# The first block's HGRN values of all heads, computed first and with tokens on partitions

## The chip, the cores and the metric

The kernel runs on one core of one Trainium2 chip. The metric is the device time of one execution in microseconds (us); the median of several runs counts. A difference of 0.2%, which is 4.8 us here, is about the least that can be told from no change. The engines go by the profile's names: PE (TensorE, with its weight loads as PEld), DVE (VectorE), ACT (ScalarE), POOL (GpSimd) and SP (SyncE, whose queue issues every DMA of this kernel).

## The reference: what is computed

One encoder layer is applied to a prompt of 512 tokens and to a sample of 1024 tokens, with 1024 channels, all in fp32. Cut to what matters here:

```python
h = rms_norm(x, n_pre_mix)                 # x * rsqrt(mean(x^2)) * gain, per token
proj = h @ w_in                            # 1024 x 6672
qkv_g, z_g, a_g, b_g, q_h, f_h, i_h, g_h, gate_raw = split(proj)
# Gated DeltaNet, 4 heads, both directions: conv + silu on q,k,v; l2norm;
#   per chunk a triangular inverse; a state that is carried over the chunks
# HGRN2, 4 heads, both directions:
ih = to_heads(i_h, HG_HEADS)               # the values v of the recurrence
# S_t = diag(f_t) S_{t-1} + k_t v_t^T,  o_t = S_t^T q_t
o_b = gla_chunked(qh, kh[0], ih, logf[0]) + flip_seq(gla_chunked(...))
merged = gates_a * (o_a @ w_br_gdn) + gates_b * (o_b @ w_br_hg)
x = x + rms_norm(merged @ w_out, n_post_mix)
h2 = rms_norm(x, n_pre_ffn)
return x + rms_norm((silu(h2 @ w_gate) * (h2 @ w_up)) @ w_down, n_post_ffn)
```

`i_h` is the projection that the change is about. It is used linearly, with no activation.

## The kernel before, in words

**Blocks.** Tokens are handled in three blocks of 512: sequence 0 is block 0 (the prompt), sequence 1 is blocks 1 and 2. K, the 1024 input channels, is cut into eight parts of 128 (`KD = 8`). A projection of 128 output columns over one block is 24 matmuls of 128x128 weights against 512 moving columns: eight parts of K by three products (`mm3`: high by high, high by low, low by high). Each fp32 operand is split into a rounded high part (an activation on ACT) and the rest (a subtraction on DVE); the helper is `split`. The result has channels on partitions and tokens in the free dimension, in one PSUM bank of eight.

**The first block.** `prelude(q)` loads the transposed input `xt` in eight parts of 256 KB, scales each by the norm's gain and splits it into `hi` and `lo` (`ha_a` in the profile). These are not yet divided by the token's root mean square. Projections that run on them are called raw: their eviction waits until the sums of squares over tokens are known (`pl.mark(("rstd", 0))`), and multiplies by the row `rstd[0]`. The sums of squares and the small decay products (`ab_products`) are 128-row, 32-column matmuls on PE; in the plan they stand behind the line `yield ("at", TOKENS)`. The activations that square the inputs (`sq`), a few constants (`constants()`, `ab_constants()`) and the splitting of the first weights share ACT and DVE with the splitting of `xt`. Weights come by `fetch`, 512 KB each; `AHEAD` says behind which part of the input the first of them are issued: z of head 0 (1536) behind part 0, q of HGRN (2064) behind part 1, the values (3600) behind part 4.

**The values before.** In `dense(q)` each head has its own projection `C_IH + h * P`, with `cbv` as its eviction: a copy of the bank to `iT`, and later `transp`, four 128x128 transposes on PE and a copy from the bank, so that tokens stand on partitions. `hg_post` uses the result (`out["v"]`) as the moving operand, `hg_mix` as weights.

**Streams.** Five generators write the program in an order that a planner (`Plan.run`) decides with its own rough clock: the prelude, the Gated DeltaNet stream (`gdn`), the HGRN stream, the dense stream (all plain projections and the 16 gate projections of a sequence), and the second phase. For each Gated DeltaNet head there is a chain: K projection, convolution on DVE, Gram matrix, a 31-step inverse on POOL (`inverse`, fed through DRAM tile `u_sc`), merges, then the recurrence. Dense projections fill PE meanwhile. Keys hold some of them back: a gate of group k needs Gated DeltaNet head k-1, and the gates past `HOLD[q][k]` of a group wait for `("inv", q, k)`, set late in the inverse of head k. `TRIG` names the inverse after which the sample's prelude starts.

**The order on the engines.** `Tape` records all operations and `schedule` orders them by a model of the engines and DMAs. On each engine, the ready operation with the lowest number comes first; an operation that is ready is never held back for a better one that isn't. The emitted order per engine is fixed; the hardware then runs each queue in that order. `URGENT` moves weight splits ahead in that numbering, `NEAR` bounds how far a matmul of the same form may be pulled ahead, `NW` is the number of buffers for split weights (4 KB a partition each). Every operation is emitted from one line of the file, so all of the trace has line 649; tiles tell the operations apart: `la_a`, `ba_a`, `sm_a`, `sa_a` hold fp32 data, `wa_a` split weights, `ha_a` split inputs, `bank` PSUM.

The second phase (branches, output projection, FFN) follows and is not touched but for `NW` and `NEAR`.

Of the kernel before, what the change touches and what calls it, by code (L numbers as in the profile page):

```python
# [13 lines left out]
F32 = mybir.dt.float32  # L14
F32R = mybir.dt.float32r
I32 = mybir.dt.int32
AF = mybir.ActivationFunctionType
# [4 lines left out]
P = 128  # L22
D = 1024
KD = D // P
# [9 lines left out]
C_Z, C_A, C_QH, C_FH, C_IH, C_GH, C_GATE = 1536, 2048, 2064, 2576, 3600, 4112, 4624  # L34
QSCALE = 128.0 ** -0.5
TBUFS = 8
NW = 6
NH = NFF // 2
MIXER = ("ones", "offd", "m_all", "m_b", "mbd", "wab0", "wab1")
RBUFS = 1  # L40
WBUFS = (2, 2, 2)
HOLD = ((2, 2, 2, 2), (2, 2, 2, 2))
MSTEP = (24, 28)
PAIR = False
SKEW = 24
URGENT = 100
PO = False
NVEC = 88
AHEAD = {0: 1536, 1: 2064, 4: 4112 - 512}
TRIG = 2  # L50
TOKENS, NORMED = 10.0, 30.0
QSQ = P * EPS ** 0.5
EPSQ = P * EPS * EPS

# [108 lines left out]
class Tape:  # L163
# [7 lines left out]
    SWITCH = 110  # L171
    FULL = (P, P)
    ENTER = 55
    NEAR = 300
    GROUP = 4
    AHEAD = 500
    RATE = 260.0
# [585 lines left out]

@with_exitstack
def layer(ctx, tc, x_p, x_s, w_out, n_post_mix, n_post_ffn, w_down, vec, xt_p, xt_s, w_in, w_br, w_gate, w_up,
          w_ab, y_p, y_s):
    tc.nc.scalar.preload_act_table_set("natural_log_exp_and_others")
    nc = Tape(tc.nc)
    w_out, w_down = w_out[0], w_down[0]
# [11 lines left out]
    def act(out, in_, func, **kw):  # L781
        nc.scalar.activation(out, in_, func, **kw)
        pl.op("ACT", out, aps(in_, kw.get("bias"), kw.get("scale")))
        if kw.get("accum_out") is not None:
            pl.ready[pl.key(kw["accum_out"])] = pl.ready[pl.key(out)]
# [20 lines left out]
    def stt(out, a, s, b, op0, op1):  # L806
        nc.vector.scalar_tensor_tensor(out, a, s, b, op0, op1)
        pl.op("DVE", out, aps(a, s, b))
# [126 lines left out]
    def h_tiles():  # L935
        return [pl.tile(hp, [P, KD, TB], F32R, n, n, 2) for n in ("h_hi", "h_lo")]
# [63 lines left out]
    def blk(name):  # L1000
        return pl.tile(tp, [P, TB + 4], F32, name, "t", TBUFS)[:, 0:TB]
# [92 lines left out]
    class Seq:  # L1094
        def __init__(self, si, b0, nb):
            self.si, self.b0, self.nb = si, b0, nb
            self.nt, self.L, self.ni = nb * 4, nb * TB, nb * 8
            self.n_i = 4 * self.ni
            self.hT = []
            self.ab = {}  # L1100
            self.late = None
            self.z = {}
            self.hg = [dict() for _ in range(HEADS)]

    def rstd_row(blk_):
# [47 lines left out]
    def prelude(q):  # L1153
        def load(b, k):
            xt = gt_("xt", 8)
            src = (xt_p if q.si == 0 else xt_s)[k * P:(k + 1) * P, b * TB:(b + 1) * TB]
            dma(xt, src)
            return xt

        def normed(b, k, xt, hi, lo, eng=None):  # L1160
            stt(xt, xt, g_mix[:, k:k + 1], rstd[q.b0 + b], ALU.mult, ALU.mult)
            split(hi[:, k, :], lo[:, k, :], xt, eng)
        if q.si == 0:
            xt = []
            for k in range(KD):
                xt.append(load(0, k))
                if k in AHEAD:
                    ahead[AHEAD[k]] = fetch(AHEAD[k])
                if k == 3:
                    for i in range(2):  # L1170
                        dma(wab[i].rearrange("p k m -> p (k m)"), w_ab[:, i * P:(i + 1) * P])
            hi, lo = h_tiles()
            for k in range(KD):
                act(hi[:, k, :], xt[k], AF.Copy, scale=g_mix[:, k:k + 1])
                stt(lo[:, k, :], xt[k], g_mix[:, k:k + 1], hi[:, k, :].bitcast(F32), ALU.mult, ALU.subtract)
            q.hT.append((hi, lo))
            pl.done["h", 0, 0] = 0.0
            constants()
            ab_constants()
            yield ("at", TOKENS)  # L1180
            sq = [blk("sq") for k in range(KD)]
            pn = px()
            for k in range(KD):
                act(sq[k], xt[k], AF.Square)
            for k in range(KD):
                for c in range(4):
                    mm(pn[32 * c:32 * c + 32, 0:P], ones[:, 0:32], sq[k][:, c * P:(c + 1) * P], k == 0, k == KD - 1)
            ab_products(q, 0, xt, range(KD))
            r = sblk("r4")
            act(r, pn[:, 0:P], AF.Ln, bias=eps_c, scale=1.0 / D)  # L1190
            act(r, r, AF.Exp, scale=-0.5)
            ab_scaled(q, 0, r)
            row = blk("row")
            tt(t4(row), r[:, None, :].to_broadcast([P, 4, P]), ident[:, 0:P:32][:, :, None].to_broadcast([P, 4, P]), ALU.mult)
            pn = px()
            nc.apart()
            mm(pn, ones, row)
            row = blk("row")
            copy(row, pn)
            q.late = rstd[0] = row  # L1200
            pl.mark(("rstd", 0))
            while waiting:
                waiting.pop(0)()
            yield ("at", NORMED)
            hi, lo = h_tiles()
            for k in range(KD):
                yield ("at", NORMED + 10 * k)
                normed(0, k, xt[k], hi, lo)
            q.hT[0] = (hi, lo)
            q.late = None  # L1210
        else:
            for b in range(q.nb):
                yield from rstd_row(q.b0 + b)
                xt = [load(b, k) for k in range(4)]
                if b:
                    yield need(("dense", 0))
                hi, lo = h_tiles()
                for k in range(KD):
                    if k % 4 == 0:
                        yield pl.at(*xt[k:k + 4])  # L1220
                        ab_products(q, b, xt, range(k, k + 4))
                    if k < 4:
                        xt.append(load(b, k + 4))
                    normed(b, k, xt[k], hi, lo)
                    yield 0
                ab_scaled(q, b)
                q.hT.append((hi, lo))
                pl.mark(("h", q.si, b))
        pl.mark(("pre", q.si))
# [427 lines left out]
    def dense(q):  # L1657
        for h in range(HEADS):
            st = q.hg[h]
            st.update({"sf0": {}, "sf1": {}, "q": {}, "v": {}})  # L1660

            def zcb(key):
                q.z[key] = {}

                def cb(ps, b):
                    s = blk("sg")
                    sigm(s, ps)
                    q.z[key][b] = ht_("zs", 2)
                    tt(q.z[key][b], ps, s, ALU.mult)
                return cb  # L1670

            def cbq(ps, b, st=st):
                s = blk("sg")
                sigm(s, ps)
                st["q"][b] = ht_("hq", 2)
                stt(st["q"][b], ps, QSCALE, s, ALU.mult, ALU.mult)

            def cbv(ps, b, st=st):
                iT = blk("sg")
                copy(iT, ps)  # L1680
                st["v"][b] = ht_("hv", 2)
                return lambda: transp(st["v"][b], iT)

            def cbf(d, st=st):
                def cb(ps, b):
                    st["sf%d" % d][b] = ht_("sf", 4)
                    sigm(st["sf%d" % d][b], ps)
                return cb

            def hgk(i):  # L1690
                return ("hg", 0, HEADS + i) if i < 0 and q.si else (("hg", q.si, i) if i >= 0 else ("h", q.si, 0))
            zk = hgk(h - 1)
            hk = hgk(h - 1 if q.si else h - 2)
            dep = ("h", q.si, 0)
            if not (h and q.si == 0):
                yield (zk, dep, ("gdn", 0, 3) if q.si else dep), C_Z + h * P, zcb(("z", h)), ("z", q.si, h)
            yield (hk, dep), C_QH + h * P, cbq, None
            yield (hk, dep), C_IH + h * P, cbv, None
            yield (hk, dep), C_FH + h * P, cbf(0), None
            yield (hk, dep), C_FH + 512 + h * P, cbf(1), ("hgin", q.si, h)  # L1700
            if h and q.si == 0:
                yield (zk, dep), C_Z + h * P, zcb(("z", h)), ("z", q.si, h)
            yield (zk, ("gdn", q.si, h) if q.si else dep), C_GH + h * P, zcb(("G", h)), ("G", q.si, h)
# [51 lines left out]
    def hg_stream():  # L1755
        for q in seqs:
            for h in range(HEADS):
                yield need(("hgin", q.si, h), ("gdn", q.si, h))
                yield from hg_attn(q, h)
                yield need(("G", q.si, h))  # L1760
                yield from hg_mix(q, h)
                pl.mark(("hg", q.si, h))
                yield 0
# [819 lines left out]
def _layouts(a):  # L2583
# [15 lines left out]
    for c in range(4):  # L2599
# [7 lines left out]
            'w_branch': np.ascontiguousarray(np.concatenate(br, axis=2)),  # L2607
            'w_gate': _tiles(np.asarray(a['w_ffn_gate'])[0]),
            'w_up': _tiles(np.asarray(a['w_ffn_up'])[0]),
            'w_ab': ab.reshape(P, KD * 32)}  # L2610


_LAY = ('vec', 'xt_prompt', 'xt_sample', 'w_in', 'w_branch', 'w_gate', 'w_up', 'w_ab')


# [13 lines left out]
```

## Time and profile before

| | |
|---|---|
| median of 3 runs | 2384.22 us (2383.85 to 2384.77) |
| profiled execution, its own time | 2382.66 us |
| span of its trace | 2381.0 us, 37933 instructions |
| PE busy | 2362.8 us (99%), 14183 matmul records |
| PEld / DVE / ACT / POOL busy | 83% / 73% / 52% / 32% |
| first matmul starts at | 8.01 us |
| last matmul group ends at | 2373.6 us |
| DMA | 42.6% of 16 engines' span, 141 GB/s |

A timeline row gives the start in us, the time in us from the first start to the last end of the rows that were merged, the engine, line and operation, the tiles written and read, the shape and the count; brackets tell how long the engine had been idle and what ended that. A waits row gives the total idle time, how often, and the longest. A windows row gives, for one stretch, each engine's busy time and instruction count, the granted PE clock, the busy share of the DMA engines and the rate. A chain row gives the start and length of a piece of the chain of waits that ended last.

### The profile page before, as it was taken

What the parts mean: (1) busy time and instruction counts of PE and PEld (TensorE: products, weight loads), DVE (VectorE), ACT (ScalarE), POOL (GpSimd) and SP (SyncE); (2) the same over time, 40 slices, a digit from 0 to 9 for tenths busy, and PEclk for the clock granted to TensorE, in tenths of its full rate; (3) what the DMA queues carried; (4) which work ended last, traced back from release to release, by engine and by line L of the source; (5) the groups of instructions that cost most, each with busy time, mean ns of one, the idle gap of its engine ahead of it and who ended that gap; (6) DMA issues with size and microseconds to landing.
All of it is one profiled execution on the core that took longest, in us unless ns stands there. A gap on an engine that the chain in (4) does not pass through costs nothing.

```text
span 2381.0 us, 37933 instructions
## 1 busy us (share of the span) xinstructions
PE 2362.8 (99%) x14183; PEld 1974.6 (83%) x14183; DVE 1727.0 (73%) x2826; ACT 1239.0 (52%) x2159; POOL 755.4 (32%) x1019
## 2 busy tenths in 40 slices
PE   8999999999999999999999999999999999999998
PEld 7888888888888888888888888888888888888887
DVE  8777898857857968758766984755887877544566
ACT  6656776746637547548442464545354444433343
POOL 0623435241602612502310011114666774200221
PEclk9999999999999999999999999999999999999999
DMA  5242643221330321324873463552454544674463
GB/s 199 95 145 63 218 143 101 95 66 46 101 96 18 100 83 54 96 78 148 299 261 133 159 221 110 163 170 84 168 192 175 187 170 160 213 246 137 148 206 125
DMA packets 193496, 337.72 MB, mean 142 GB/s; under 512 B 53185, under 2 KB 92961, under 8 KB 193313
## 3 DMA queue, kind: packets, MB, share of 16 engines
q1 hardware_dynamic: 193312, 335.31, 42.6%
q8 instruction: 111, 1.82, 0.3%
q14 instruction: 73, 0.59, 0.1%
HBM read 254.59 MB, written 80.66 MB: 141 GB/s over the span
## 4 chain that ended last, share of the span: by engine, by line
PE 90%; DVE 2%; DMA 1%; ACT 1%; SPq 0%; issue 0%; POOL 0%; DVEq 0%; ACTq 0%; POOLq 0%
PE bank L649 90%; DVE la_a L649 1%; DMA ba_a<-lay_w_in 1%; DVE ba_a L649 1%; ACT la_a L649 0%; SPq L649 0%; DMA ba_a<-x_sample 0%; DVE wa_a L649 0%; ACT ba_a L649 0%; ACT wa_a L649 0%; DMA dram_g_sc<-la_a 0%; ACT sm_a L649 0%; DMA la_a<-dram_u_sc 0%; DVE sm_a L649 0%; POOL la_a L649 0%
## 5 line engine op out<-in xcount | busy, mean ns | idle before, releaser
L649 PE MATMUL bank<-ha_a,wa_a 128*128 128x512 f32 x5424 | 1307.7, 395 | 8.4 <-ACT wa_a L649 8.0
L649 PEld LDWEIGHTS bank<-ha_a,wa_a 128*128 128x128 f32 x5424 | 1003.7, 188 | 210.1 <-ACT wa_a L649 8.0
L649 PE MATMUL bank<-xr_a 128*128 128x512 f32 x1386 | 314.3, 389 | 0.0
L649 PEld LDWEIGHTS bank<-xr_a 128*128 128x128 f32 x1386 | 260.1, 188 | 54.0
L649 PE MATMUL bank<-xr_a,ha_a 128*128 128x512 f32 x1200 | 275.3, 389 | 0.0
L649 PEld LDWEIGHTS bank<-xr_a,ha_a 128*128 128x128 f32 x1200 | 225.2, 188 | 46.8
L649 POOL TENSOR_TENSOR ba_a<-ba_a 128x512 f32<-128x512 f32 (+1 forms) x123 | 159.8, 1305 | 219.0 <-ACT wa_a L649 79.9
L649 ACT ACTIVATE la_a<-la_a 128x512 f32<-128x512 f32 (+1 forms) x307 | 194.4, 649 | 42.5 <-DVE la_a L649 30.7
L649 DVE TENSOR_TENSOR wa_a<-la_a,wa_a 128x1024 fp32r<-128x1024 f32 (+1 forms) x121 | 142.0, 1184 | 59.7 <-PE bank L649 28.3
L649 ACT ACTIVATE wa_a<-la_a 128x1024 fp32r<-128x1024 f32 (+1 forms) x121 | 118.3, 986 | 106.2 <-PE bank L649 97.7
L649 DVE TENSOR_TENSOR wa_a<-ba_a,wa_a 128x1024 fp32r<-128x1024 f32 (+1 forms) x103 | 123.6, 1218 | 68.7 <-PE bank L649 57.5
L649 ACT ACTIVATE wa_a<-ba_a 128x1024 fp32r<-128x1024 f32 (+1 forms) x103 | 99.3, 980 | 118.5 <-PE bank L649 94.9
L649 ACT ACTIVATE ha_a<-ba_a 128x512 fp32r<-128x512 f32 (+1 forms) x126 | 80.7, 642 | 135.7 <-PE bank L649 109.9
L649 POOL TENSOR_TENSOR la_a<-la_a 128x256 f32<-128x256 f32 (+1 forms) x80 | 89.4, 1133 | 183.1 <-DVE la_a L649 67.9
L649 DVE TENSOR_TENSOR ha_a<-ba_a,ha_a 128x512 fp32r<-128x512 f32 (+1 forms) x126 | 127.9, 1020 | 13.4 <-ACT ha_a L649 12.8
L649 DVE TENSOR_TENSOR la_a<-la_a 128x512 f32<-128x512 f32 (+2 forms) x193 | 126.2, 669 | 12.6 <-ACT la_a L649 11.6
L649 POOL TENSOR_TENSOR la_a<-la_a,sm_a 128x30 f32<-128x30 f32 (+43 forms) x248 | 124.6, 502 | 18.3
L649 POOL TENSOR_TENSOR sm_a<-la_a 128x126 f32<-128x126 f32 (+37 forms) x155 | 79.8, 515 | 133.2 <-DMA la_a<-dram_u_sc 104.4
L649 PE MATMUL bank<-wa_a,ha_a 128*128 128x512 f32 x528 | 120.1, 389 | 0.0
L649 DVE TENSOR_TENSOR xr_a<-da_a,xr_a 128x1024 fp32r<-128x1024 f32 (+2 forms) x60 | 71.2, 1200 | 64.1 <-ACT xr_a L649 44.0
L649 ACT ACTIVATE ba_a<-ba_a 128x512 f32<-128x512 f32 (+1 forms) x164 | 104.6, 648 | 24.0 <-DVE ba_a L649 16.7
L649 PEld LDWEIGHTS bank<-wa_a,ha_a 128*128 128x128 f32 x528 | 99.0, 188 | 20.5
(205 smaller groups left out, 3305.0 us busy)
## 6 DMA issues: line engine op xcount, KB each, us to landing
la_a<-lay_w_in SPq DMA_DIRECT2D x67, 512.0 KB
ba_a<-lay_w_in SPq DMA_DIRECT2D x37, 512.0 KB
ba_a<-lay_w_gate SPq DMA_DIRECT2D x35, 512.0 KB
ba_a<-lay_w_up SPq DMA_DIRECT2D x34, 512.0 KB
dram_a_sc<-xa_a SPq DMA_DIRECT2D x56, 256.0 KB
ba_a<-w_ffn_down SPq DMA_DIRECT2D x24, 512.0 KB
da_a<-dram_a_sc SPq DMA_DIRECT2D x22, 512.0 KB
ba_a<-dram_a_sc SPq DMA_DIRECT2D x20, 512.0 KB
```

What stands on the lines that cost most here:

```text
L649: f(*[m(a) for a in o.args], **{k: m(a) for k, a in o.kw.items()})
```

## The change

The values of all four heads of block 0 are computed in `prelude`, as the first thing emitted for PE, with `hi`/`lo` of the input as weights (128 tokens each) and a new weight layout `w_ih` (K by all 512 value columns) as the moving operand. For each part of K, a 256 KB tile of `w_ih` is loaded behind its input part, split on ACT and DVE, and used in 12 matmuls into four banks `pv`, one per 128 tokens. When the root mean squares `r` are known, one transpose of `r` gives them per partition (`rc`), and four activations scale the banks into `q.v`, tokens on partitions. The four `C_IH` projections of sequence 0 with their evictions and transposes are gone. Sequence 1 keeps them. Constants: `NW` 6 to 7, one `HOLD` entry 2 to 1, `URGENT` 100 to 150, `NEAR` 300 to 400, `AHEAD` now K of head 0 (512), z (1536) and q (2064) behind parts 4, 6 and 7, `TRIG` 2 to 0, `TOKENS` 10 to 22.

```diff
-NW = 6
+NW = 7
-HOLD = ((2, 2, 2, 2), (2, 2, 2, 2))
+HOLD = ((2, 2, 1, 2), (2, 2, 2, 2))
-URGENT = 100
+URGENT = 150
-AHEAD = {0: 1536, 1: 2064, 4: 4112 - 512}
-TRIG = 2
-TOKENS, NORMED = 10.0, 30.0
+AHEAD = {4: 512, 6: 1536, 7: 2064}
+VSPLIT = 4
+TRIG = 0
+TOKENS, NORMED = 22.0, 30.0
-    NEAR = 300
+    NEAR = 400
...
         if q.si == 0:
             xt = []
+            hi, lo = h_tiles()
+            pv = [px() for t in range(4)]
+            wr = []
             for k in range(KD):
                 xt.append(load(0, k))
+                wr.append(blk("wv"))
+                dma(wr[k], w_ih[k])
                 if k in AHEAD:
                     ahead[AHEAD[k]] = fetch(AHEAD[k])
...
-            hi, lo = h_tiles()
-            for k in range(KD):
+            def values(k):
                 act(hi[:, k, :], xt[k], AF.Copy, scale=g_mix[:, k:k + 1])
+                hl = pl.tile(wsp, [P, 1024], F32R, "whl", "whl", 6)
+                wh, wl = hl[:, 0:TB], hl[:, TB:2 * TB]
+                split(wh, wl, wr[k])
                 stt(lo[:, k, :], xt[k], g_mix[:, k:k + 1], hi[:, k, :].bitcast(F32), ALU.mult, ALU.subtract)
+                for x, w in ((hi, wh), (hi, wl), (lo, wh)):
+                    for t in range(4):
+                        mm(pv[t], x[:, k, t * P:(t + 1) * P], w, k == 0 and w is wh and x is hi, k == KD - 1 and x is lo)
+            for k in range(VSPLIT):
+                values(k)
             q.hT.append((hi, lo))
             pl.done["h", 0, 0] = 0.0
             constants()
             ab_constants()
+            for k in range(VSPLIT, KD):
+                values(k)
+                yield 0
             yield ("at", TOKENS)
...
             ab_scaled(q, 0, r)
+            pc = px()
+            tr(pc[:, 0:P], r)
+            rc = sp.tile([P, 4], F32, name="rc", tag="rc", bufs=1)
+            vcopy(rc, pc[:, 0:P:32])
+            q.v = pl.tile(gp, [P, 4 * TB], F32, "vall", "vall", 1)
+            for t in range(4):
+                act(q.v.rearrange("p (h t c) -> p h t c", t=4, c=P)[:, :, t, :], t4(pv[t]), AF.Copy, scale=rc[:, t:t + 1])
...
-            yield (hk, dep), C_IH + h * P, cbv, None
+            if q.si:
+                yield (hk, dep), C_IH + h * P, cbv, None
...
+                if q.v is not None:
+                    q.hg[h]["v"][0] = q.v[:, h * TB:(h + 1) * TB]
...
+            'w_ih': np.ascontiguousarray(w[:, C_IH:C_IH + HEADS * P].reshape(KD, P, HEADS * P))}
```

More of the change, by code (lines that the diff above doesn't have):

```diff
@@ L765, in layer @@
 def layer(ctx, tc, x_p, x_s, w_out, n_post_mix, n_post_ffn, w_down, vec, xt_p, xt_s, w_in, w_br, w_gate, w_up,
-          w_ab, y_p, y_s):
+          w_ab, w_ih, y_p, y_s):
     tc.nc.scalar.preload_act_table_set("natural_log_exp_and_others")
@@ L1102, in __init__ @@
             self.z = {}
+            self.v = None
             self.hg = [dict() for _ in range(HEADS)]
@@ L2609, in _layouts @@
             'w_up': _tiles(np.asarray(a['w_ffn_up'])[0]),
-            'w_ab': ab.reshape(P, KD * 32)}
-_LAY = ('vec', 'xt_prompt', 'xt_sample', 'w_in', 'w_branch', 'w_gate', 'w_up', 'w_ab')
+            'w_ab': ab.reshape(P, KD * 32),
+            'w_ih': np.ascontiguousarray(w[:, C_IH:C_IH + HEADS * P].reshape(KD, P, HEADS * P))}
+_LAY = ('vec', 'xt_prompt', 'xt_sample', 'w_in', 'w_branch', 'w_gate', 'w_up', 'w_ab', 'w_ih')
 def kernel(**inputs):
```

## The prediction

> **What bounds the kernel now.** I read first the busy shares on the page, then what PE waited for, then the stretches of the span, then the chain of waits. The page and the waits of PE over the whole span:
>
> ```profile
> span 2381.0 us, 37933 instructions
> PE 2362.8 (99%) x14183; PEld 1974.6 (83%) x14183; DVE 1727.0 (73%) x2826; ACT 1239.0 (52%) x2159; POOL 755.4 (32%) x1019
> ...
> PE bank L649 <- ACT wa_a L649: 9.1, 4, 8.0
> PE bank L649 <- DVE la_a L649: 0.6, 1, 0.6
> ```
>
> PE has work for all but 18.2 us, and 8.0 of these are one wait, the first. The stretches tell where the others are, and that the busy time is dense:
>
> ```profile
> 8.00:12.00 4.00, 3.95 (x9) 2.61 (x10) 3.80 (x5) 4.00 (x7) 0.00 (x0) 1.00 1.05 399
> 12.00:16.00 4.00, 4.00 (x19) 3.29 (x18) 2.45 (x5) 4.00 (x7) 0.00 (x0) 1.00 1.04 417
> 24.50:410.00 385.50, 382.83 (x2778) 317.03 (x2776) 320.64 (x606) 261.86 (x479) 159.26 (x345) 1.00 0.38 122
> 410.00:2373.50 1963.50, 1963.44 (x11235) 1644.59 (x11233) 1389.35 (x2172) 959.93 (x1648) 592.50 (x646) 1.00 0.44 143
> 2373.50:2381.00 7.50, 0.05 (x1) 0.00 (x0) 3.35 (x8) 1.22 (x4) 0.00 (x0) 0.77 0.19 70
> 2100.00:2200.00 100.00, 100.00 (x443) 82.78 (x442) 46.40 (x47) 35.17 (x38) 0.00 (x0) 1.00 0.51 162
> ```
>
> 443 matmuls of 512 columns in 100 us are 0.226 us each; call it 0.227. Idle: 8.0 at the start, 2.67 between 24.5 and 410, 0.06 in the 1963 us behind that, and 7.45 at the end, which the change doesn't touch. So the time is the sum of PE's instructions plus some 18 us. A change that moves no matmul out can gain from the first wait, from the 2.67 us, and from instructions it deletes; no more. It can lose wherever PE runs dry.
>
> **The change, part by part.** *The matmuls.* Before: 4 heads x 24 = 96 matmuls of 512 columns. After: 8 parts x 3 products x 4 token tiles = 96 of the same shape. At 0.227 both are 21.8 us. Sum 0.
>
> *The transposes.* One group of four, as PE ran it:
>
> ```profile
> 37.63 2.88 PE L649 MATMUL bank<-ha_a,wa_a 128*128 128x512 f32 x12
> 40.35 0.60 PE L649 MATMUL bank<-sa_a,la_a 128*128 128x128 f32 x4
> 40.71 3.67 PE L649 MATMUL bank<-ha_a,wa_a 128*128 128x512 f32 x15
> ```
>
> A lone record of 512 columns lasts 0.39 us (12 of them at 0.227 apart end 2.88 us behind the first start: 2.88 - 11 x 0.227 = 0.38). The last of the 15 thus starts at 40.71 + 3.67 - 0.39 = 43.99. From 37.63 to the end of its slot at 44.22 are 6.59 us, of which 27 matmuls take 6.13. The group costs 0.46 us, 0.115 a transpose. Four groups go and one transpose (of `r`) comes: -15 x 0.115 = -1.7 us, all on PE and so all in the sum.
>
> *The first wait.* What PE waited for, on each queue:
>
> ```profile
> 1.24 0.42 SPq L649 DMA_DIRECT2D la_a<-lay_xt_prompt  x1
> 1.71 0.43 SPq L649 DMA_DIRECT2D la_a<-lay_w_in  x1
> ...
> 3.00:4.00 1.00, 0.00 (x0) 0.00 (x0) 0.96 (x4) 0.00 (x0) 0.96 (x10) 1.00 1.05 338
> 4.00:5.00 1.00, 0.00 (x0) 0.00 (x0) 0.92 (x6) 0.00 (x0) 0.56 (x4) 1.00 0.99 403
> ...
> 5.67 0.21 ACT L649 ACTIVATE sa_a<-sa_a 128x8 f32<-128x8 f32 x1 [2.82 <-DVE sa_a L649]
> 5.78 0.70 ACT L649 ACTIVATE ha_a<-la_a,sa_a 128x512 fp32r<-128x512 f32 x1
> 6.40 0.61 ACT L649 ACTIVATE la_a<-la_a 128x512 f32<-128x512 f32 x1
> 6.92 1.04 ACT L649 ACTIVATE wa_a<-la_a 128x1024 fp32r<-128x1024 f32 x1
> ...
> 6.70 0.75 DVE L649 SCALAR_TENSOR_TENSOR ha_a<-la_a,sa_a,ha_a 128x512 fp32r<-128x512 f32 x1
> 7.99 1.23 DVE L649 TENSOR_TENSOR wa_a<-la_a,wa_a 128x1024 fp32r<-128x1024 f32 x1 [0.54 <-ACT wa_a L649]
> ...
> 8.01 4.45 PE L649 MATMUL bank<-ha_a,wa_a 128*128 128x512 f32 x9 [8.01 <-ACT wa_a L649]
> ```
>
> The reader is to see that the weight isn't what ACT stood idle for. ACT sat 2.82 us in front of a small constant (128x8) that DVE released at 5.67. Behind it come the first input part (5.78), a square of that part (6.40), and only then the high part of the weight, which ends at 7.96; PE follows 0.05 later. The change halves the first weight (256 KB), but the constant is emitted by the same code for the same queues, and the schedule takes whatever is ready: with both loads at the same places of SP's queue, the constant again stands ahead of the first input part and I expect the square again ahead of the weight. What is left is the width: 512 columns take 0.61 (the 6.40 row) where 1024 took 1.04. The weight's high part then runs 6.92 to 7.53 and PE starts at 7.58, 0.43 sooner. The low part of the weight, half as wide, is on DVE by 8.3; four matmuls come before it is needed, so it doesn't hold PE as the 7.99 row did. Bounds: no gain (the order on ACT gets worse by one square, 0.5) and 2.46, if nothing stands ahead: 307 KB for the constants and the first part have moved within about 4 us by the 338 and 403 GB/s rows, the weight's 256 KB take 0.6 more, and 0.6 each on ACT for input and weight give a start near 5.55. I take the value that the ACT rows give.
>
> The first matmuls are slow: 9 records in 8 to 12, 19 in the next 4 us, so some 2.3 us are lost whatever runs there. With the granted clock shown as 1.00 in both rows I take the loss as unchanged and moved along with the start. Without the wait on the weight's low part the gain is 0.5 in all.
>
> By the Trainium skill ("TensorE: Matmul & The Clock Gate", Part 1: The HAM clock gate) the array starts at half clock and is released after a busy window of about 3.4 us that runs freely, so that the number of slow matmuls differs from run to run. By that rule an earlier start may be worth anything from nothing to its whole length, and an estimate from the page's counts of 6 to 14 slow ones is 1 us to either side. The trace agrees that the slow stretch ends near 12 us; one execution can't show its spread.
>
> *Feeding the values.* Each part needs 512 KB (1.3 us at 400 GB/s), on ACT 0.70 + 0.61 + a square of 0.61, on DVE 0.75 + 0.67 (the input's difference and, at the rate of the 1.23 row, the weight's), and on PE 12 x 0.227 = 2.72. Nothing but PE bounds it. If the fetch were late by a part, 1.3 us would show; 2 MB are in flight, so I cost it at 0. SP issues 8 loads more early and 4 fetches fewer later; the input's last part lands near 15 us and is used after 28.
>
> *What is moved back.* Before, the sums of squares ran at 20.1:
>
> ```profile
> 20.13 0.64 PE L649 MATMUL bank<-la_a,sm_a 128*32 128x128 f32 x16
> ...
> 21.90 1.93 PE L649 MATMUL bank<-la_a,sm_a 128*32 128x128 f32 x64
> ...
> 24.10 1.02 PE L649 MATMUL bank<-la_a,sm_a 128*128 128x512 f32 x2
> ```
>
> After, values end at 7.58 + 4.0 (nine) + 87 x 0.227 = 31.3. The planner's clock reads 20.5 there and `TOKENS` is 22, so half of z goes first (12 x 0.227 = 2.7) and the sums start near 34, 14 us later. The row of 24.1 comes near 38. Until then the raw results of z and K sit in PSUM: four banks of values, the sums, the decay products, z and K are eight of eight. The other half of z and K, 8.1 us of PE work, cover the 4 us from the sums to the row (20.13 to 24.10). If that cover were gone, it costs 4 us. The new scaling chain (transpose, a copy, four activations of some 0.6) is first used by HGRN, far behind. Evictions and copies that go (8 activations of 0.6, four of a 1.04 and a 1.23) were off the path; ACT is busy for 52%.
>
> *The Gated DeltaNet chain.* With the sums 14 us later, the inverse starts later:
>
> ```profile
> 66.12 1.22 POOL L649 TENSOR_TENSOR sm_a<-la_a,ba_a 128x31 f32<-128x31 f32 x1 [26.14 <-DMA ba_a<-dram_u_sc]
> ...
> 24.50:62.00 37.50, 37.50 (x174) 30.94 (x173) 37.39 (x64) 26.41 (x53) 1.70 (x2) 1.00 0.29 89
> ...
> 99.38 3.80 SPq L649 DMA_DIRECT2D dram_g_sc<-la_a  x2
> ...
> 107.67 0.21 POOL L649 TENSOR_TENSOR la_a<-la_a,sm_a 128x8 f32<-128x8 f32 x1
> ```
>
> From 24.5 to 62 DVE is full (37.39 of 37.5), so the way from sums to inverse can't shrink much: it starts between 66 and 80, and I take 76, since K is now the first projection. The gates 0 and 1 are the last fill before the inverse of head 0 releases more; their results leave from 99 to 103. The values of heads 2 and 3 come in addition ahead of that point: 48 x 0.227 = 10.9 us of fill against some 10 us of delay. About even. Heads 1 and 2 then each have one projection (5.45 us) less to fill with; the sample's prelude, now behind inverse 0, gives 2 to 3 us back (32-column products and the small row products). I take the idle between 24.5 and 410 as unchanged, 2.67, with ends of 0 and about 11 more.
>
> The remaining constants: `NW` and `URGENT` act on splits that PE waited 1.5 us for; `NEAR` changes which group of small matmuls runs first, and entering such a group costs nothing in the three rows of the transposes. 0 each.
>
> *The sum.* -0.5 - 1.7 = -2.2. The profiled execution took 2382.66, so 2380.4; the median of the runs stands 1.6 above it, so 2382.0.
>
> **The rivals.** *Faster: the start comes clear of the constant.* If the order on ACT puts the first input part and the small weight ahead of the constant and the square, PE starts near 5.55 (-2.5). With the transposes that is -4.2, and half of the 2.67 gone makes -5.5: 2378.7. For it: both loads would be there by 5; ACT had nothing to do for 2.82 us. Against it: the constant's queue position follows from code that isn't touched ahead of that time.
>
> *Slower: PE runs dry in the inverses of heads 1 and 2.* Its place is where the chain of waits leaves PE:
>
> ```profile
> 127.46 10.07 PE bank L649 x68
> 154.91 7.26 DMA ba_a<-lay_w_in
> 164.34 67.00 PE bank L649 x423
> ...
> 246.16 7.99 DMA ba_a<-x_sample
> 257.18 44.54 PE bank L649 x256
> ...
> 404.38 15.72 PE bank L649 x204
> ```
>
> Between 137 and 164 and between 231 and 257 the path runs over DMA and other engines while PE lives on fill; one projection less in each is 2 x 5.45 = 10.9, less the gain: +8.7, 2392.9. It decides from about 7 us of new idle. For it: the fill was just enough (0.06 us idle behind 410, but 2.67 before). Against it: in 164 to 231 and 257 to 302 the path is PE itself, so less work there lets the chain go on sooner.
>
> *It doesn't do what it says*: z or K runs first after all and the values wait. Their weights are issued behind parts 4 to 7, so this needs the small weight to come after 2.5 MB; 0.02, inside the likeliest.
>
> **How the numbers follow.** Likeliest, 0.57: -2.2 with idle within 2 us or so of before, own range 2379.5 to 2387. Faster rival and its like, 0.25. Slower rival, 0.18. 0.2% is 4.8 us, about what can be told from no change here: the likeliest lies within it, the rivals outside on their sides. The range of 2377.5 to 2390 leaves about 0.1 on each side.
>
> **What would show it.** First matmul at 7.6 and no transposes for values; a 128x8 activation still ahead of the first input part on ACT; sums of squares near 34; first inverse operation on POOL near 76; idle of PE between 24.5 and 410 near 2.7. A first matmul below 6, or idle there above 7, makes the prediction wrong.

## Result and the profile after

The changed kernel takes 2376.24 us (median of 7 runs, 2375.66 to 2377.54) against 2384.22 us (median of 7, 2383.39 to 2384.77) before: a ratio of 0.9968, 95% interval 0.9957 to 0.9978. That is 8.0 us less, faster by more than 0.2%, and 1.3 us below the low end of the predicted range. The profiled execution took 2376.19 us.

The busy shares on the page of the changed kernel, and its chain by engine:

```profile
span 2374.5 us, 37882 instructions
...
PE 2359.3 (99%) x14168; PEld 1974.5 (83%) x14168; DVE 1722.2 (73%) x2826; ACT 1244.3 (52%) x2159; POOL 753.7 (32%) x1019
...
PE 98%; DVE 1%; ACT 0%; issue 0%; POOL 0%; DVEq 0%; POOLq 0%
```

Exactly 15 PE records are gone (14183 to 14168): sixteen transposes less and one more. The chain that ended last is PE for 98% of the span. The waits of PE over the whole span of the changed kernel (waited for: us in total, times, longest):

```profile
PE bank L650 <- ACT wa_a L650: 7.5, 1, 7.5
PE bank L650 <- DVE wa_a L650: 0.2, 1, 0.2
```

Behind the wait for the first weight almost nothing is left. Where that was gained shows in the stretches of the changed kernel (PE busy and count are the first pair behind the width of the stretch; the clock is third from the end):

```profile
8.00:12.00 4.00, 4.00 (x11) 3.09 (x11) 3.43 (x6) 4.00 (x9) 0.00 (x0) 1.00 1.02 385
12.00:16.00 4.00, 4.00 (x19) 3.31 (x18) 2.85 (x7) 4.00 (x7) 0.14 (x2) 1.00 1.04 400
24.50:410.00 385.50, 385.35 (x2918) 321.69 (x2917) 320.80 (x619) 264.87 (x480) 158.66 (x345) 1.00 0.38 124
410.00:2366.00 1956.00, 1955.79 (x11185) 1638.27 (x11184) 1383.72 (x2158) 959.80 (x1642) 591.45 (x646) 1.00 0.43 144
```

PE is idle for 0.15 us of the 385.5 in which the prediction kept 2.67. The start and the steps that the prediction named, on the timeline of the changed kernel:

```profile
5.63 0.21 ACT L650 ACTIVATE sa_a<-sa_a 128x8 f32<-128x8 f32 x1 [2.71 <-DVE sa_a L650]
5.75 0.71 ACT L650 ACTIVATE ha_a<-la_a,sa_a 128x512 fp32r<-128x512 f32 x1
6.36 0.61 ACT L650 ACTIVATE la_a<-la_a 128x512 f32<-128x512 f32 x1
6.88 0.61 ACT L650 ACTIVATE wa_a<-la_a 128x512 fp32r<-128x512 f32 x1
...
7.55 24.04 PE L650 MATMUL bank<-wa_a,ha_a 128*128 128x512 f32 x96 [7.55 <-ACT wa_a L650]
...
19.58 0.33 SPq L650 DMA_DIRECT2D ba_a<-x_sample  x1
...
31.52 0.64 PE L650 MATMUL bank<-la_a,sm_a 128*32 128x128 f32 x16
...
36.76 1.02 PE L650 MATMUL bank<-la_a,sm_a 128*128 128x512 f32 x2
...
81.25 0.42 POOL L650 TENSOR_TENSOR sm_a<-la_a,ba_a 128x31 f32<-128x31 f32 x1 [23.36 <-DMA ba_a<-dram_u_sc]
```

The start came out as drawn: the 128x8 constant ahead of the first input part, the square ahead of the weight, the weight's high part in 0.61, PE at 7.55. The 96 matmuls of the values run in one row without a wait. The long pieces of the chain of waits of the changed kernel:

```profile
7.55 145.17 PE bank L650 x941
...
179.50 135.46 PE bank L650 x959
314.96 79.78 PE bank L650 x655
394.79 753.76 PE bank L650 x5578
```

Between 231 and 257 the chain before ran over ACT and a load of `x_sample`. Now it stays on PE from 179.5 to 1148. With `TRIG` 0 the eight loads of `x_sample` for this prelude leave between 19.58 and 82.82, the first of them long ahead of the first inverse operation (81.25); before, they left between 227.24 and 267.63.

### The profile page after: what moved, and what is told of

Same layout as the page of the kernel before. It is cut to its first block, busy times and chain, and to the rows that moved or that the text cites. A ratio compares the mean times of both kernels' runs of the same rounds, so it can differ in the third digit from the quotient of the medians.

```text
span 2374.5 us, 37882 instructions
## 1 busy us (share of the span) xinstructions
PE 2359.3 (99%) x14168; PEld 1974.5 (83%) x14168; DVE 1722.2 (73%) x2826; ACT 1244.3 (52%) x2159; POOL 753.7 (32%) x1019
## 4 chain that ended last, share of the span: by engine, by line
PE 98%; DVE 1%; ACT 0%; issue 0%; POOL 0%; DVEq 0%; POOLq 0%
PE bank L650 98%; DVE la_a L650 1%; DVE ba_a L650 0%; DVE wa_a L650 0%; ACT la_a L650 0%; ACT wa_a L650 0%; DVE da_a L650 0%; DVE sm_a L650 0%; POOL sm_a L650 0%; DVE sa_a L650 0%; POOL la_a L650 0%; ACT ba_a L650 0%; DVEq L2653 0%; ACT ha_a L650 0%; POOL sa_a L650 0%
## 5 line engine op out<-in xcount | busy, mean ns | idle before, releaser
L650 PE MATMUL bank<-ha_a,wa_a 128*128 128x512 f32 x5328 | 1278.7, 394 | 0.0
L650 PEld LDWEIGHTS bank<-ha_a,wa_a 128*128 128x128 f32 x5328 | 985.1, 188 | 196.5 <-issue 1.3
L650 ACT ACTIVATE la_a<-la_a 128x512 f32<-128x512 f32 (+1 forms) x324 | 204.9, 647 | 56.8 <-DVE la_a L650 42.5
L650 PE MATMUL bank<-wa_a,ha_a 128*128 128x512 f32 x624 | 144.2, 393 | 7.5 <-ACT wa_a L650 7.5
L650 DVE TENSOR_TENSOR la_a<-la_a 128x512 f32<-128x512 f32 (+2 forms) x200 | 138.4, 705 | 12.2 <-ACT la_a L650 11.5
L650 PEld LDWEIGHTS bank<-wa_a,ha_a 128*128 128x128 f32 x624 | 118.5, 190 | 32.2 <-ACT wa_a L650 7.5
L650 POOL TENSOR_TENSOR la_a<-la_a 128x256 f32<-128x256 f32 (+1 forms) x63 | 62.8, 1011 | 172.2 <-DVE la_a L650 79.4
L650 ACT ACTIVATE xr_a<-da_a 128x1024 fp32r<-128x1024 f32 (+2 forms) x60 | 58.5, 987 | 106.2 <-PE bank L650 105.9
L650 PE MATMUL bank<-ha_a 128*128 128x512 f32 x480 | 112.1, 389 | 0.0
L650 PEld LDWEIGHTS bank<-ha_a 128*128 128x128 f32 x480 | 90.2, 188 | 18.6
```

The costliest lines, as they stand in the source:

```text
L650: f(*[m(a) for a in o.args], **{k: m(a) for k, a in o.kw.items()})
```

## Experiments

Each was run beside the kernel before on the same chip (its median there 2383.75 to 2384.49). All have an interval. "Idle" is PE's idle time behind 24 us and ahead of the tail, in the profiled execution; "slow start" counts matmuls of 512 columns among the first 48 that were over 0.4 us apart.

| kernel | median, us | ratio to before (95%) | first matmul | slow start | idle, us |
|---|---|---|---|---|---|
| before, first profile | 2384.22 | 1 | 8.01 | 8 | 2.73 |
| after | 2376.24 | 0.9968 (0.9957–0.9978) | 7.55 | 9 | 0.36 |
| e1 before again | 2384.04 | 1.0002 (0.9993–1.0011) | 8.01 | 8 | 4.33 |
| e2 after, all five constants old | 2388.90 | 1.0023 (1.0014–1.0032) | 7.55 | 13 | 9.05 |
| e3 before, all five new | 2383.56 | 0.9999 (0.9991–1.0008) | 8.01 | 9 | 4.08 |
| e5 after, `TRIG` 2 | 2388.51 | 1.0016 (1.0007–1.0025) | 7.56 | 13 | 7.71 |
| e6 after, `HOLD` old | 2377.19 | 0.9970 (0.9958–0.9981) | 7.41 | 8 | 1.30 |
| e13 after, `NW` 6 | 2380.18 | 0.9985 (0.9976–0.9994) | 7.55 | 14 | 2.56 |
| e14 after, `URGENT` 100 | 2384.98 | 1.0004 (0.9995–1.0012) | 7.55 | 13 | 6.41 |
| e15 after, `NEAR` 300 | 2377.88 | 0.9975 (0.9965–0.9984) | 7.55 | 12 | 2.61 |
| e10 after, old but `TRIG` 0 | 2387.92 | 1.0016 (1.0007–1.0024) | 7.40 | 12 | 7.55 |
| e11 before, only `TRIG` 0 | 2389.84 | 1.0024 (1.0015–1.0034) | 8.01 | 14 | 6.47 |
| e12 after, 64 transposes more | 2382.07 | 0.9989 (0.9980–0.9998) | 7.40 | 12 | 0.45 |
| e4 after, start clear, a column more | 2387.04 | 1.0014 (1.0005–1.0022) | 5.55 | 6 | 1.56 |
| e8 after, 88 unused columns | 2386.51 | 1.0011 (1.0002–1.0020) | 7.56 | 9 | 0.33 |
| e7 after, start clear, same addresses | 2377.42 | 0.9971 (0.9960–0.9981) | 5.57 | 9 | 2.19 |
| e9 start clear, order else kept | **2374.58** | 0.9958 (0.9945–0.9970) | 5.61 | 14 | 0.09 |

### Is it the values or the constants? e1, e2, e3

e1 is the kernel before unchanged. e2 and e3 swap the five constants between the two kernels:

```diff
e2, in the changed kernel:      e3, in the kernel before:
-NW = 7                         -NW = 6
+NW = 6                         +NW = 7
-HOLD = ((2, 2, 1, 2), ...      -HOLD = ((2, 2, 2, 2), ...
+HOLD = ((2, 2, 2, 2), ...      +HOLD = ((2, 2, 1, 2), ...
-URGENT = 150                   -URGENT = 100
+URGENT = 100                   +URGENT = 150
-TRIG = 0                       -TRIG = 2
+TRIG = 2                       +TRIG = 0
-    NEAR = 400                 -    NEAR = 300
+    NEAR = 300                 +    NEAR = 400
```

Expected of e1:

> The kernel before, unchanged, profiled once more: how far the stalls of PE and the span differ between two executions of the same program. The first profile had 2.67 us of idle PE between 24.5 and 410 us and took 2382.66, 1.6 us under the median. If that execution was lucky in a wait, this one shows a span near 2382.5 with some 4 us idle there. If the difference lies in the first microseconds (the slow matmuls), the idle in the middle is again near 2.7 and more matmuls are slow at the start. Ratio 1.000.

Expected of e2:

> The changed kernel with NW 6, HOLD, URGENT 100, NEAR 300 and TRIG 2 as before; the values stay first. Theory A (the five constants took the idle time of PE away): idle between 24.5 and 410 is 2.5 us or more again, the time 2379 to 2381. Theory B (the values as early fill took it away): idle stays under 1 us, the time 2376 to 2377.

Expected of e3:

> The kernel before with the five new constants and its values where they were. Theory A: idle between 24.5 and 410 falls below 1 us, the time is 2380 to 2381. Theory B: idle stays at 2.7 or grows, the time 2384 or more.

The waits and a stretch of e1, and three pieces of its chain:

```profile
PE bank L649 <- ACT wa_a L649: 11.0, 4, 8.0
PE bank L649 <- DVE la_a L649: 0.6, 1, 0.6
```

```profile
24.50:410.00 385.50, 381.32 (x2771) 315.84 (x2770) 319.75 (x603) 261.98 (x477) 158.11 (x345) 1.00 0.37 122
```

```profile
247.20 8.54 DMA ba_a<-x_sample
255.80 0.94 issue
258.77 44.50 PE bank L649 x256
```

The kernel before idles for 4.18 us in that stretch in this execution, not 2.67: PE came back at 258.77 behind a load of `x_sample` that took 8.54, where the first profile has 7.99 and 257.18. The first profile was an execution quicker than all seven timed ones (2382.66 against 2383.39 to 2384.77), and the idle that could be gained was read 1.6 us too small from it.

The swap shows that neither half makes the gain, and neither theory said so. The moved values with the old constants are 4.9 us slower than e1, with 9.05 us of idle; the new constants without the moved values change nothing that can be told (2383.56). `AHEAD` and `TOKENS` stayed with the moved values in all these runs, so their part isn't separated. The stretches of e2:

```profile
24.50:410.00 385.50, 380.08 (x2859) 314.33 (x2859) 317.55 (x597) 258.66 (x473) 163.61 (x345) 1.00 0.38 122
410.00:2366.00 1956.00, 1952.37 (x11185) 1634.50 (x11184) 1381.25 (x2159) 954.77 (x1637) 584.87 (x644) 1.00 0.43 143
```

PE is idle there for 5.42 us in the early stretch, nearly all of it at 181 to 185 and 401 to 407, and for 3.63 us behind 410. The stretches of e3:

```profile
24.50:410.00 385.50, 383.64 (x2795) 319.69 (x2795) 320.01 (x612) 263.35 (x479) 153.20 (x345) 1.00 0.38 122
410.00:2373.50 1963.50, 1961.28 (x11217) 1641.14 (x11216) 1389.11 (x2169) 961.38 (x1646) 585.95 (x646) 1.00 0.44 143
```

Idle in the early stretch falls from 4.18 to 1.86, but 2.22 open behind 410, where e1 has 0.15. Only the two together leave 0.36.

### Which constant? e5, e6, e10, e11, e13, e14, e15

One constant put back into the changed kernel at a time, and `TRIG` alone on either side:

```diff
e5:  -TRIG = 0       e6:  -HOLD = ((2, 2, 1, 2), ...   e13: -NW = 7   e14: -URGENT = 150   e15: -NEAR = 400
     +TRIG = 2            +HOLD = ((2, 2, 2, 2), ...        +NW = 6        +URGENT = 100        +NEAR = 300
e10: as e2, but TRIG = 0                                e11: the kernel before with TRIG = 0
```

Expected of e5:

> The changed kernel with TRIG 2 alone as before: the sample's prelude starts behind the inverse of head 2 again, not of head 0. Theory C (the sample's loads and its small products behind inverse 0 fill the holes that the moved values leave): the loads of the sample come near 230 to 270 again, PE stands still 1 to 3 us between 160 and 410, the time is 2377.5 to 2379.5. Theory D (the idle belongs to no single constant; any change of the order draws it anew): idle anywhere from 0.3 to 9 us, not tied to the places where the sample's loads are waited for.

Expected of e6:

> The changed kernel with the old HOLD alone: in the group of head 2 two gates are free before the inverse's key and not one. Theory C: without the held gate the stretch behind the inverse of head 2 runs short by one projection, 5.45 us of fill, and idle of 0.5 to 3 us shows between 290 and 410. Theory D: idle as likely elsewhere.

In e5 the idle has one main place. Its timeline there, on PE and ACT:

```profile
280.69 13.16 PE L650 MATMUL bank<-ha_a,wa_a 128*128 128x512 f32 x56
297.79 8.48 PE L650 MATMUL bank<-ha_a,wa_a 128*128 128x512 f32 x23 [3.94 <-ACT wa_a L650]
...
293.89 0.60 ACT L650 ACTIVATE la_a<-bank 128x512 f32<-128x512 f32 x1 [3.42 <-PE bank L650]
...
295.15 1.04 ACT L650 ACTIVATE ba_a<-ba_a 128x1024 f32<-128x1024 f32 x1
...
296.70 1.04 ACT L650 ACTIVATE wa_a<-la_a 128x1024 fp32r<-128x1024 f32 x1
```

ACT stood 3.42 us for a PE bank, and when it came, an eviction, two operations of 512 columns, a square of a 1024-wide sample tile (1.04) and only then the weight split ran. That weight's load had landed at 292.3, 4.4 us before its split began. PE waited 3.94 us for the split. The sample's prelude is work on ACT's queue that a weight split has to stand behind; with `TRIG` 2 its loads leave between 240 and 287 and its squares fall here. The square is some 1.1 of the 3.94 us, and the rest is the order of the other work on that queue; no run takes the two apart. Theory C had the place, but e5 is 9 us above its time. The stall costs more than its length, as the stretches of e5 behind it show:

```profile
298.00:302.00 4.00, 3.96 (x9) 2.66 (x10) 4.00 (x12) 3.24 (x5) 0.00 (x0) 0.50 0.57 201
302.00:306.00 4.00, 4.00 (x15) 3.17 (x15) 3.90 (x8) 0.00 (x0) 2.66 (x2) 0.79 0.00 0
```

Nine matmuls in 4 us at a granted clock of 0.50, where 17.6 fit at 0.227. e6 has three short waits of 1.1 us in sum, two near 225 and one at 814 and none where theory C put it (290 to 410), and 0.95 us more in the median, less than the intervals can tell.

Expected of e10:

> The changed kernel with TRIG 0 as the only new constant; NW 6, HOLD, URGENT 100, NEAR 300 as before. Theory E (of the constants it is TRIG that counts, because the sample's loads, squares and splits then don't stand in the short stretches of heads 1 to 3): idle 0.4 to 2 us, the time 2376 to 2378. Rival F (each constant takes away a part): idle 3 us or more, the time 2379 or more.

Expected of e11:

> The kernel before with TRIG 0 alone. Theory E: the waits of 127 to 360 us (near 3 us in the two profiles of the kernel before) go, and what stays or comes lies behind 390 us; the time is 2381 to 2384. If TRIG works only together with the moved values, the waits before 360 stay and the time is 2384 or more.

`TRIG` is needed, but is not the gain. The stretches of e11, and PE where it waited longest:

```profile
24.50:410.00 385.50, 384.72 (x2816) 320.32 (x2809) 322.30 (x617) 264.73 (x483) 155.80 (x346) 1.00 0.39 123
410.00:2373.50 1963.50, 1957.82 (x11189) 1639.00 (x11188) 1383.51 (x2156) 955.46 (x1642) 590.01 (x646) 1.00 0.43 143
```

```profile
1331.48 4.84 PE L649 MATMUL bank<-wa_a,ha_a 128*128 128x512 f32 x13 [4.01 <-ACT ha_a L649]
```

In the kernel before, an earlier sample prelude takes the early idle from 4.18 to 0.78, and 5.68 us open far behind, 4.01 of them at 1331, in front of an input split. e10 has a wait of 3.4 us for the same split at 1330.7. So what was gained at 160 to 360 was lost again 1000 us later, and another constant, or several together, must close that place. Rival F had e10 right (7.55 us of idle, 2387.92). The next three runs asked which.

Expected of e13:

> The changed kernel with NW back at 6, all else as changed. Theory W (the seventh buffer for split weights is what takes away the waits near 1155 and 1316 to 1331): PE idle behind 24 us of 4 us or more, with a wait above 1 us in 1310 to 1340, and a median of 2383 to 2388. Theory M (the idle belongs to the whole order; any one constant put back opens some wait, at a place of its own): idle of 1 to 6 us, not at those places, median 2377 to 2384. Theory N (another constant): idle below 1 us, median 2376 +- 1.

Expected of e14:

> The changed kernel with URGENT back at 100. Theory U (moving weight splits further ahead is what takes the waits away): PE idle behind 24 us of 4 us or more, with a wait above 1 us in 1310 to 1340, median 2383 to 2388. Theory W: idle below 1 us, median 2376 +- 1. Theory M: idle of 1 to 6 us at other places.

Expected of e15:

> The changed kernel with NEAR back at 300. Theory N3 (how far a matmul of the same form is pulled ahead decides): PE idle behind 24 us of 4 us or more with a wait above 1 us in 1310 to 1340, median 2383 to 2388. Theory W: idle below 1 us, median 2376 +- 1, and short waits in front of groups of 128x128 matmuls up by no more than 1 us. Theory M: idle of 1 to 6 us at other places.

Every one of the three opens waits. e13 has its main one near the place in question, but for another operand:

```profile
1314.11 0.63 PE L650 MATMUL bank<-sa_a,ba_a 128*128 128x128 f32 x4 [1.67 <-DVE ba_a L650]
```

e14 is the surprise, 8.7 us slower than the changed kernel, in waits that are all short. Its waits of PE:

```profile
PE bank L650 <- ACT wa_a L650: 8.7, 4, 7.6
PE bank L650 <- DVE wa_a L650: 2.6, 4, 1.1
PE bank L650 <- DVE ba_a L650: 1.7, 3, 0.7
PE bank L650 <- DVE la_a L650: 0.8, 1, 0.8
```

Behind the first wait these are eleven, from 180 to 1414 us, seven of them for a weight's high or low part, none above 1.1 us, none near 1331. Theory U had e14's idle (6.41) and time right, and the place wrong. e15 has 2.61 us of idle, the longest wait 1.07 at 1157, and a median 1.6 us up. That a single constant closes the place from 1310 to 1340 thus failed for `URGENT` and `NEAR`; for `NW` the place fits and the wait does not, and its median (2380.18) falls short of the 2383 that was expected. What fits all of them best is that the idle belongs to the whole order. The five changes put back one at a time cost 12.3 (`TRIG`), 8.7 (`URGENT`), 3.9 (`NW`), 1.6 (`NEAR`) and 1.0 (`HOLD`); all at once they cost 12.7. Only the first two are clear of the changed kernel's interval, and these two alone make 21.0. They don't add.

### What is a transpose worth? e12

The first 16 groups of four transposes of the changed kernel run twice, in place:

```diff
     order = nc.schedule()
+    ...
+    for g in groups[:16]:
+        at_ = order.index(g[-1]) + 1
+        order[at_:at_] = g
```

Expected of e12:

> The changed kernel with the first 16 groups of four transposes run twice in place (same inputs, same bank, so the result is the same): 64 more 128x128 transposes on PE, nothing else. If PE's instructions are the time, 64 x 0.111 to 0.115 = 7.1 to 7.4 us more: 2383.5. If PE has slack that hides them, less. That prices the 15 transposes that the change removed: 1.7 us.

The same place on the timeline of e12, and of the changed kernel:

```profile
66.21 1.04 PE L650 MATMUL bank<-sa_a,la_a 128*128 128x128 f32 x8
```

```profile
65.90 0.60 PE L650 MATMUL bank<-sa_a,la_a 128*128 128x128 f32 x4
```

64 transposes cost 5.83 us of median, 0.091 each, and not the 7.1 to 7.4 expected; these rows say 0.11 for each of four more (1.04 less 0.60). Most of the cost arrives in the time, so PE has no slack in which they would hide; why 0.11 in the rows becomes 0.091 in the time stays open. At that price the 15 of the change are worth 1.4 us, not 1.7.

### What is the start worth? e4, e8, e7, e9

e4 loads the first weight part ahead of the first input part and takes the late constant (the lower-bound logits, the 128x8 operation) from a second load behind the fourth input part:

```diff
                 xt.append(load(0, k))   # for k = 0 now behind the weight's load
+    vcol2 = ctile([P, NVEC], "vcol2")
-    lbl = vcol[:, 18:26]
+    lbl = vcol2[:, 18:26]
...
+                    dma(vcol2, vec)     # at k == 3
```

Expected of e4:

> The changed kernel, with the first weight part loaded ahead of the first input part, and the lower-bound constants fed from a second load of the small vector behind input part 3, so that nothing stands ahead of them on ACT. If the start is set by the order on ACT, as in the prediction, the first matmul starts near 5.6 (7.55 in the changed kernel) and the time falls by some 1.9 us to 2374.3. If the loads set it, the start stays above 7. If the slow stretch of PE ends at a fixed time whatever starts it, less than 1.9 us comes through.

The start moved by 2.0 us as drawn, the idle stayed small, and yet the median rose by 10.8 us. The loss lay 1600 us later. Matmuls with `xr_a` there, and `ha_a` or `wa_a` on the other side, stood 234.2 ns apart (mean) instead of 226.7. The new column had moved the tiles behind it by 352 bytes a partition. e8 does only that:

```diff
     rst2 = ctile([P, 12], "rst2")
+    ctile([P, NVEC], "spare")
```

Expected of e8:

> The changed kernel with 88 unused columns reserved among the constants (352 bytes a partition): every queue holds the same instructions in the same order, only addresses move. If addresses set the pace of the FFN's matmuls, those with one operand in the split tiles of the last phase and the other in the split inputs take 234 ns, about 1320 x 7.4 ns = 9.8 us, and the time is 2386. If they don't, 2376.

The stretch from 1700 to 1800 us in e8, and the same in the changed kernel:

```profile
1700.00:1800.00 100.00, 100.00 (x432) 80.94 (x431) 78.87 (x94) 39.39 (x66) 66.08 (x45) 1.00 0.47 166
```

```profile
1700.00:1800.00 100.00, 100.00 (x443) 82.87 (x442) 81.13 (x96) 40.28 (x67) 69.15 (x46) 1.00 0.47 165
```

PE is busy throughout in both at the same clock, with 11 matmuls fewer in 100 us. An unused tile costs 10.3 us: 1298 such matmuls at 7.5 ns more are 9.7 of them. e7 has the clear start with the logits loaded into a tile that was already there; e9 leaves all loads and every order as in the changed kernel, puts the seven operations on the logits behind the fourth input part, and the first square behind the first weight split:

```diff
e7: +    lbl = noml
    +                    dma(noml, vec[:, 18:26])    # at k == 3, first weight ahead of first input as in e4
e9:      order = nc.schedule()
    +    ...
    +    order[at_:at_] = late_ops
    +    order.remove(sq0)
    +    order.insert(order.index(wh0) + 1, sq0)
```

Expected of e7:

> The clear start once more, with the lower-bound logits loaded into a column that exists already, so that no address moves. First matmul near 5.6. If the loss in the run with the second vector came from the addresses (matmuls with weights and columns in the split inputs and in the FFN's split tiles took 234 ns and not 227 there), these take 227 again and the time is 2374 to 2376, less or more by whatever idle the new order draws. If it came from the clear start, the time stays above 2384.

Expected of e9:

> The changed kernel with its order on every queue kept, except that the seven lower-bound operations stand behind the fourth input part and the first square behind the first weight split. Theory (the start is set by ACT's order alone, and the idle of PE by the rest of the order): first matmul near 5.5, idle behind it below 0.6 us as in the changed kernel, the time 2374.2, 2 us less. Rival (the slow matmuls of the start end at a fixed time): first matmul near 5.5 but only some 1 us through, 2375.2.

In e7 the start is 2.0 us earlier and the median is 1.2 us higher: the two loads moved the schedule, and 2.19 us of idle opened at seven places (151 to 1156 us). e9, on its timeline, keeps both:

```profile
3.72 0.72 ACT L650 ACTIVATE ha_a<-la_a,sa_a 128x512 fp32r<-128x512 f32 x1 [0.75 <-DMA la_a<-lay_xt_prompt]
4.93 0.63 ACT L650 ACTIVATE wa_a<-la_a 128x512 fp32r<-128x512 f32 x1 [0.48 <-DMA la_a<-lay_w_ih]
...
5.61 24.93 PE L650 MATMUL bank<-wa_a,ha_a 128*128 128x512 f32 x96 [5.61 <-ACT wa_a L650]
```

PE starts 1.94 us earlier and idles for 0.09. It is the fastest of all: 2374.58 us, 1.7 below the changed kernel (the intervals of the two ratios overlap). The profiled span gains 1.2, for the 96 matmuls take 24.93 us here and 24.04 there: 14 slow ones against 9. By themselves these two traces would fit the rival of e9, for the slow matmuls end at 11.75 here and at 11.92 there. But in e4 and e7, which start as early, they end at 8.6 and 9.9, so their end isn't fixed.

## Why the prediction was wrong

By its own steps:

- **The matmuls, 0; the feeding, 0.** Right. The 96 run in one row, and 8 to 16 us show PE full.
- **The first wait, -0.5.** Right, with its mechanism: 7.55 against 7.58 predicted.
- **The transposes, -1.7.** Right in kind, a little large: 15 at 0.091 are 1.4.
- **The slow first matmuls, unchanged.** They were 9 here and 8 before, so nearly unchanged, but 6 to 14 over the 17 traces: the first 40 matmuls lost between 1.5 and 3.4 us against a pace of 0.227, which is the 1 us to either side that the prediction drew from the Trainium skill.
- **What is moved back.** The sums start at 31.52, not near 34: no half of z ran ahead. The row matmul came at 36.76 (38 predicted), with other matmuls in between.
- **The Gated DeltaNet chain.** The first inverse operation came at 81.25, 15 us later than before, 5 later than the 76 taken and past the 80 that was its end, and with the new constants that cost PE nothing.
- **The idle between 24.5 and 410, "unchanged, 2.67". This step failed**, with the one behind it, the constants at "0 each". The base was off (4.18 in the other execution of the kernel before), and the term went to 0.15. The working priced the constants by what PE had waited for in the kernel before: splits were worth at most 1.5 us there. Measured in the changed kernel, putting `URGENT` back costs 8.7, and `TRIG`, which had been allowed "2 to 3 us" of fill, 12.3. With the old constants the moved values do cost idle (e2: 9.05 us, 2388.90), but not as the slower rival had it: 5.42 us of it lie between 24.5 and 410, below the 7 from which it decides, and next to none at its places, 137 to 164 and 231 to 257. The constants close these waits and the ones of the kernel before too.
- **Entering a group of small matmuls, "costs nothing".** This failed as well. The three rows of the prediction happened to show an entry on time. In e1, 47 of the 212 entries from 512 columns into a group of 128x128 records came more than 0.04 us late.

Against e1 the span fell by 7.5 us: 0.46 from the start, 0.1 in the first 40 matmuls (one more slow one, but no wait for a weight's low part), 0.1 at the end, 1.4 from the transposes and 3.97 of idle. The other 1.5 agree in size with waits too short to show as idle: these entries took 4.0 us above a pace of 0.233 in all in e1 and 2.1 in the changed kernel, worked out from the start-to-start times in the two traces with the idle taken off. `NEAR`, to which the prediction tied this cost, isn't what lowered it: with `NEAR` at 300 in e15 the same sum is 1.8. It is 3.6 in e2 and 2.7 in e3, so it too goes with the whole order. That these entries are the missing 1.5 us is argued, not tested.

The faster rival had the sign and, with half of the idle gone in its sum, a part of the cause; but its main term didn't come: the start did not come clear of the constant. e9 shows what that would have been worth, some 1.7 us.

**Open.** Why putting a given constant back opens a wait at a given place is not settled, and in e5 only in part; which pair of them closes the wait at 1331 that e10 and e11 share wasn't tried.

## What to carry to other kernels

Where one engine is busy for 99% and the rest is a schedule, price a change of order and its constants together: one half alone may gain nothing or cost time, and the single effects don't add. Don't bound a priority constant by the waits of the kernel before; it is worth the waits that the change would otherwise open, so look for the queue on which they would form (in e5 it was ACT, with an eviction and a sample square ahead of a weight split). Take the idle from more than one execution, and keep tiles at their addresses when an experiment adds one.

## What the runs showed of the hardware

**Addresses set the pace of a matmul.** 352 bytes a partition more ahead of them, and matmuls of 512 columns on `xr_a` with `ha_a` or `wa_a` go from 226.7 to 234.2 ns, at a granted clock of 1.00 (e8, e4). In e8 ACT, DVE and POOL run the same instructions in the same order as in the changed kernel. With the old addresses the pace is back (e7). Which operand's address matters wasn't tried.

**A stall brings the slow clock back.** The 3.94 us of e5 was followed by 4 us at a granted 0.50, the 4.01 of e11 by 0.57 and the 3.36 of e10 by 0.61. In e2 two waits, 1.68 and 0.70 us within 3.1 us, did it too:

```profile
183.06 0.73 PE L650 MATMUL bank<-ha_a,wa_a 128*128 128x512 f32 x2 [1.68 <-ACT wa_a L650]
184.49 4.71 PE L650 MATMUL bank<-ha_a,wa_a 128*128 128x512 f32 x13 [0.70 <-ACT wa_a L650]
```

```profile
184.50:188.50 4.00, 4.00 (x11) 3.18 (x12) 4.00 (x9) 3.07 (x4) 2.77 (x5) 0.61 1.03 405
```

A single wait of 1.76 us (e1, at 258.77) or 1.67 us (e13) did not, and neither did four waits of 2.82 us in all within 5.6 us in e14 (397 to 403). So the sum of the idle alone doesn't decide. At the start of the kernel the profile shows a granted 1.00 while the first matmuls run 0.427 apart, so the pace is the safer sign. The Trainium skill ("TensorE: Matmul & The Clock Gate", Part 1: The HAM clock gate) has the array fall back to half clock behind an idle window of about 3.4 us. The stalls of 3.94, 4.01 and 3.36 agree; in e2 the idle was 2.38 us in two parts, less than such a window, and the clock fell all the same. The same section of the Trainium skill says that the number of slow first matmuls differs from run to run, with counts of 6, 11 and 14; these runs, of different kernels, show 6 to 14.
